# Moving the fp32-to-bf16 casts of x from GpSimd to VectorE in a scaled matrix product

## The chip, the core and the metric

The kernel runs on one core of a Trainium2 chip. The metric is the device time of one execution in microseconds (us). Before the change the median of three runs was 218.16 us (218.0 to 218.54).

## The reference

```python
batch, m, k, n = 16, 512, 1024, 768        # x: batch,m,k; weight: k,n; add_value: batch,m,n; scale 0.1; all float32
def reference(x, weight, scale, add_value):
    return (scale * np.matmul(x, weight) + add_value).astype(np.float32)
```

All batches share one weight, so this is one product of 8192 x 1024 with 1024 x 768, scaled, plus an addend of the size of the result.

## The kernel before, in words

**Tiles.** The 8192 rows are cut into T = 64 tiles of 128 rows (row number p * 64 + t is partition p of tile t, so that several tiles in a row are one contiguous piece per partition). [...]

**Memory.** `xs` is a ring of 24 slots for x tiles in fp32 (512 KB each), `ao` a ring of 24 slots for tiles of add_value (384 KB each); the result overwrites the addend in its slot and is stored from there. The weights are staged in the last eight slots of `ao` before the addends need them (L79), and kept in `w_bf` as bf16. There are four buffers for casts (`xb`), three for transposed tiles (`xt`), two for transposes in PSUM (`tp`) and three for products in PSUM (`mm`).

**What happens to one tile t.**
- It is cast from fp32 to bf16, `xb` from `xs` (L87), by `cast_to`.
- TensorE transposes it in four pieces (L97). Pairs of neighbouring bf16 values are treated as one 4-byte value, so four 128x128 transposes against an fp32 identity move the 1024 columns.
- ScalarE copies the transposes out of PSUM into `xt` and sorts the pairs apart (L99).
- TensorE does 16 matmuls into `mm` (L114): 4 chunks by 2 members of a pair by 2 column pieces.
- VectorE computes `ao` = scale * `mm` + `ao` in one instruction (L118), called the add below.
- SyncE stores `ao` (L144), usually four tiles at a time.

**What sets the order.** The instructions stand in each engine's queue in the order in which the program emits them, and each engine takes its queue in order. `STREAM` (L11 to L23) is the written order of all DMAs, all on SyncE's queue: loads of x ("x"), weights ("w"), add_value ("a") and stores ("o"), with first tile and number of tiles. The loop over it (L127) emits the work of tiles only when it is needed: before a store, all steps up to its last tile (`steps_to`), and before a load of x into a slot that is still in use, steps until the old tile there has been cast. The four weight loads and their casts on VectorE (`load_w`, L81) are emitted at once when the loop meets them, and the first steps come only with the store ("o", 0, 4).

`step` (L103) emits one tile's matmuls. After the first half of its chunks it calls `transpose(t + 1)`, so that the transposes and the copy of the next tile lie within the matmuls of this one; `transpose` calls `cast_to` for its tile (L92). The casts are on GpSimd, whose queue holds nothing else after the identity matrix is made, so that they run ahead of TensorE as far as the loads and the four `xb` buffers let them.

Of the kernel before, what the change touches and what calls it, by code (L numbers as in the profile page):

```python
# [1 line left out]

# [5 lines left out]

STREAM = [  # L11
    ("x", 0, 1), ("w", 0, 1), ("w", 1, 1), ("w", 2, 1), ("w", 3, 1), ("x", 1, 1),
    ("x", 2, 2), ("a", 0, 4), ("x", 4, 4), ("a", 4, 4), ("x", 8, 4), ("a", 8, 4),
    ("x", 12, 4), ("a", 12, 4), ("x", 16, 4), ("a", 16, 4), ("x", 20, 4), ("o", 0, 4),
    ("a", 20, 4), ("x", 24, 4), ("o", 4, 4), ("a", 24, 4), ("x", 28, 4), ("o", 8, 4),
    ("a", 28, 4), ("x", 32, 4), ("o", 12, 4), ("a", 32, 4), ("x", 36, 4), ("o", 16, 4),
    ("a", 36, 4), ("x", 40, 4), ("o", 20, 4), ("a", 40, 4), ("x", 44, 4), ("o", 24, 4),
    ("a", 44, 4), ("x", 48, 4), ("o", 28, 4), ("a", 48, 4), ("x", 52, 4), ("o", 32, 4),
    ("a", 52, 4), ("x", 56, 2), ("o", 36, 4), ("x", 58, 2), ("a", 56, 2), ("x", 60, 1),
    ("a", 58, 2), ("x", 61, 1), ("o", 40, 4), ("x", 62, 1), ("a", 60, 1), ("x", 63, 1),  # L20
    ("a", 61, 1), ("a", 62, 1), ("a", 63, 1), ("o", 44, 4), ("o", 48, 4), ("o", 52, 4),
    ("o", 56, 2), ("o", 58, 2), ("o", 60, 1), ("o", 61, 1), ("o", 62, 1), ("o", 63, 1),
]  # L23

X_SLOTS = 24
A_SLOTS = 24


@with_exitstack
def kernel(  # L30
    ctx: ExitStack,
    tc: tile.TileContext,
    x: bass.AP,
    weight: bass.AP,
    scale: float,
    add_value: bass.AP,
    out: bass.AP,
):
    nc = tc.nc
    P = 128  # L40
    bf16 = mybir.dt.bfloat16
    fp32 = mybir.dt.float32

    x_f = x.flatten_outer_dims()
    add_f = add_value.flatten_outer_dims()
    out_f = out.flatten_outer_dims()
    M, K = x_f.shape
    _, N = weight.shape
    T = M // P
    KC = K // (2 * P)  # L50

    x_v = x_f.rearrange("(p t) k -> p t k", p=P)
    add_v = add_f.rearrange("(p t) n -> p t n", p=P)
    out_v = out_f.rearrange("(p t) n -> p t n", p=P)

    w_v = weight.rearrange("(c p r) n -> p c r n", p=P, r=2)

    const = ctx.enter_context(tc.tile_pool(name="const", bufs=1))
    xb_pool = ctx.enter_context(tc.tile_pool(name="xb_pool", bufs=4))
    xt_pool = ctx.enter_context(tc.tile_pool(name="xt_pool", bufs=3))  # L60
    tp_pool = ctx.enter_context(
        tc.tile_pool(name="tp_pool", bufs=2, space=bass.MemoryType.PSUM))
    mm_pool = ctx.enter_context(
        tc.tile_pool(name="mm_pool", bufs=3, space=bass.MemoryType.PSUM))
    ctx.enter_context(tc.manual_schedule())

    identity = const.tile([P, P], fp32, name="identity")
    make_identity(nc, identity)
    xs = const.tile([P, X_SLOTS, K], fp32, name="xs")
    ao = const.tile([P, A_SLOTS, N], fp32, name="ao")  # L70
    w_bf = const.tile([P, KC, 2, N], bf16, name="w_bf")

    SPLITS = [(0, 512), (512, N)]

    xb_tiles, xt_tiles, done = {}, {}, {"cast": 0, "step": 0}

    def load_w(c):

        s = A_SLOTS - 2 * KC + 2 * c  # L79
        nc.sync.dma_start(ao[:, s:s + 2, :], w_v[:, c, :, :])  # L80
        nc.vector.tensor_copy(w_bf[:, c, :, :], ao[:, s:s + 2, :])  # L81

    def cast_to(t):
        while done["cast"] <= t:
            i = done["cast"]
            xb = xb_pool.tile([P, K], bf16, tag="xb")
            nc.gpsimd.tensor_copy(xb, xs[:, i % X_SLOTS, :])  # L87
            xb_tiles[i] = xb
            done["cast"] += 1

    def transpose(t):
        cast_to(t)  # L92

        pairs = xb_tiles.pop(t).bitcast(fp32)
        tp = tp_pool.tile([P, KC, P], fp32, tag="tp")
        for c in range(KC):
            nc.tensor.transpose(tp[:, c, :], pairs[:, c * P:(c + 1) * P], identity)  # L97
        xt = xt_pool.tile([P, KC, 2, P], bf16, tag="xt")
        nc.scalar.copy(  # L99
            xt, tp.bitcast(bf16).rearrange("p c (m r) -> p c r m", r=2))  # L100
        xt_tiles[t] = xt

    def step():  # L103
        t = done["step"]
        if t == 0:
            transpose(0)
        xt = xt_tiles.pop(t)
        mm = mm_pool.tile([P, 1024], fp32, tag="mm")
        for c in range(KC):
            if c == KC // 2 and t + 1 < T:  # L110
                transpose(t + 1)
            for r in range(2):
                for n0, n1 in SPLITS:
                    nc.tensor.matmul(  # L114
                        mm[:, n0:n1], xt[:, c, r, :], w_bf[:, c, r, n0:n1],
                        start=(c == 0 and r == 0), stop=(c == KC - 1 and r == 1))
        a = ao[:, t % A_SLOTS, :]
        nc.vector.scalar_tensor_tensor(  # L118
            a, mm[:, 0:N], float(scale), a,
            op0=mybir.AluOpType.mult, op1=mybir.AluOpType.add)  # L120
        done["step"] += 1

    def steps_to(t):
        while done["step"] <= t:
            step()

    for op, s, n in STREAM:  # L127
        if op == "w":
            load_w(s)
            continue  # L130
        last = s + n - 1
        if op == "x":
            if last >= X_SLOTS:
                while done["cast"] <= last - X_SLOTS:
                    step()
            k = s % X_SLOTS
            nc.sync.dma_start(xs[:, k:k + n, :], x_v[:, s:s + n, :])  # L137
        elif op == "a":
            k = s % A_SLOTS
            nc.sync.dma_start(ao[:, k:k + n, :], add_v[:, s:s + n, :])  # L140
        else:
            steps_to(last)
            k = s % A_SLOTS
            nc.sync.dma_start(out_v[:, s:s + n, :], ao[:, k:k + n, :])  # L144


# [1 line left out]
_INS = ['x', 'weight', 'scale', 'add_value']  # L148
_OUTS = [((16, 512, 768), 'float32')]

_NUMBERS = {'scale': 0.10000000149011612}


# [26 lines left out]
```

## Time and profile before

| what | value |
|---|---|
| median of three runs | 218.16 us |
| the profiled execution's own time | 218.0 us |
| its span, first to last instruction | 216.2 us |
| ScalarE copies (L99) | 64, mean 1012 ns |
| loads of x, 2 MB each | median 20.7 us from issue to landing |
| loads of add_value, 1.5 MB each | median 15.9 us |
| stores, 1.5 MB each | median 23.5 us |
| bytes moved | 87.23 MB, 403 GB/s over the span |

How to read it: engines are PE (TensorE's matmuls and transposes), PEld (its weight loads, beside PE), DVE (VectorE), ACT (ScalarE), POOL (GpSimd) and SP (SyncE). The page gives the busy time and the number of instructions of each engine; the span in 40 slices, each digit the busy share in tenths; the chain that ended last, which goes back from the last instruction to whatever released it, by engine and line; and groups of instructions, each with its line, engine, operation, output <- inputs, shape and count, then busy us, mean ns of one, and the idle time of the engine before them with what ended it. A row of the timeline is start us, duration us, engine, line, operation, and in brackets the idle time before it and its releaser. A row of the chain in order of time is start us, duration us, engine and line. In the slices, the DMA engines and PE are both nearly full:

```profile
PE   0739999999999999999999999999999999999991
DVE  0521333233323332233223323332233223332331
POOL 3032526162333233233332333233323332331000
PEclk9999999999999999999999999999999999999997
DMA  6999999999999999999999999999999999999733
```

### The profile page before, as it was taken

What the parts mean: (1) busy time and instruction counts of PE and PEld (TensorE: products, weight loads), DVE (VectorE), ACT (ScalarE), POOL (GpSimd) and SP (SyncE); (2) the same over time, 40 slices, a digit from 0 to 9 for tenths busy, and PEclk for the clock granted to TensorE, in tenths of its full rate; (3) what the DMA queues carried; (4) which work ended last, traced back from release to release, by engine and by line L of the source; (5) the groups of instructions that cost most, each with busy time, mean ns of one, the idle gap of its engine ahead of it and who ended that gap; (6) DMA issues with size and microseconds to landing.
All of it is one profiled execution on the core that took longest, in us unless ns stands there. A gap on an engine that the chain in (4) does not pass through costs nothing.

```text
span 216.2 us, 3116 instructions
## 1 busy us (share of the span) xinstructions
PE 200.2 (93%) x1255; PEld 124.6 (58%) x1280; DVE 65.1 (30%) x68; ACT 66.1 (31%) x65; POOL 66.8 (31%) x70
## 2 busy tenths in 40 slices
PE   0739999999999999999999999999999999999991
PEld 0325665666566656666666566656666666666650
DVE  0521333233323332233223323332233223332331
ACT  2112223322333233323332333233323332333220
POOL 3032526162333233233332333233323332331000
PEclk9999999999999999999999999999999999999997
DMA  6999999999999999999999999999999999999733
GB/s 229 421 430 430 430 422 445 412 427 417 433 434 421 432 428 426 420 430 435 422 422 436 420 433 419 446 411 435 419 436 420 416 421 421 418 434 418 303 121 146
DMA packets 9518, 87.23 MB, mean 403 GB/s; under 512 B 1056, under 2 KB 1056, under 8 KB 3872
## 3 DMA queue, kind: packets, MB, share of 16 engines
q1 hardware_dynamic: 9504, 87.04, 95.6%
q8 instruction: 10, 0.16, 0.3%
q14 instruction: 4, 0.03, 0.0%
HBM read 61.87 MB, written 25.17 MB: 403 GB/s over the span
## 4 chain that ended last, share of the span: by engine, by line
PE 90%; DMA 4%; SPq 1%; issue 1%; POOL 0%; ACT 0%; DVE 0%; ACTq 0%
PE mm L114 77%; PE tp L97 13%; DMA xs<-in_x_dram 4%; SPq L80 1%; POOL xb L87 0%; ACT xt L99 0%; DVE ao L118 0%; SPq L137 0%; ACTq L99 0%
## 5 line engine op out<-in xcount | busy, mean ns | idle before, releaser
L114 PE MATMUL mm<-w_bf,xt 128*128 128x512 bf16 (+1 forms) x999 | 181.2, 329 | 2.6 <-ACT xt L99 1.3
L114 PEld LDWEIGHTS <-xt 128*128 128x128 bf16 x1024 | 96.1, 99 | 69.8 <-ACT xt L99 16.9
L99 ACT COPY xt<-tp 128x1024 bf16<-128x1024 bf16 x64 | 64.8, 1012 | 142.3 <-PE tp L97 142.3
L87 POOL CAST xb<-xs 128x1024 bf16<-128x1024 f32 x64 | 66.1, 1041 | 129.4 <-PE tp L97 97.4
L118 DVE SCALAR_TENSOR_TENSOR ao<-mm,ao 128x768 f32<-128x768 f32 x64 | 61.3, 957 | 138.8 <-PE mm L114 132.3
L97 PE MATMUL tp<-identity,xb 128*128 128x128 f32 x256 | 39.4, 278 | 9.1 <-POOL xb L87 9.1
L97 PEld LDWEIGHTS tp<-identity,xb 128*128 128x128 f32 x256 | 30.4, 143 | 17.1 <-POOL xb L87 9.8
L81 DVE CAST w_bf<-ao 128x1536 bf16<-128x1536 f32 x4 | 3.8, 959 | 9.0 <-DMA ao<-in_weight_dram 9.0
L99 ACT ACT_TABLE_LOAD x1 | 1.3, 1283 | 0.7 <-PEq L161 0.7
masks.py:199 POOL TENSOR_SCALAR_AFFINE_SELECT identity<-identity 128x128 f32<-128x128 f32 x1 | 0.3, 292 | 0.1
masks.py:197 POOL MEMSET identity<- 128x128 f32 x1 | 0.2, 204 | 0.3 <-POOLq L161 0.3
L161 POOL MEMSET const-float32-0.0<- 128x1 f32 x1 | 0.1, 98 | 0.2 <-issue 0.2
L161 POOL MEMSET const-bfloat16-1.0<- 128x1 bf16 x1 | 0.1, 101 | 0.0
L161 POOL MEMSET const-uint8-127<- 128x1 uint8 x1 | 0.1, 101 | 0.0
L161 POOL MEMSET const-float32-1.0<- 128x1 f32 x1 | 0.1, 98 | 0.0
## 6 DMA issues: line engine op xcount, KB each, us to landing
xs<-in_x_dram SPq DMA_DIRECT2D x13, 2048.0 KB, 20.7
ao<-in_add_value_dram SPq DMA_DIRECT2D x14, 1536.0 KB, 15.9
out_dram<-ao SPq DMA_DIRECT2D x14, 1536.0 KB, 23.5
xs<-in_x_dram SPq DMA_DIRECT2D x6, 512.0 KB, 14.8
ao<-in_weight_dram SPq DMA_DIRECT2D x4, 768.0 KB, 7.1
xs<-in_x_dram SPq DMA_DIRECT2D x3, 1024.0 KB, 17.8
ao<-in_add_value_dram SPq DMA_DIRECT2D x2, 768.0 KB, 15.3
ao<-in_add_value_dram SPq DMA_DIRECT2D x4, 384.0 KB, 13.4
```

Of the source, the lines that this page charges most:

```text
L80: nc.sync.dma_start(ao[:, s:s + 2, :], w_v[:, c, :, :])
L81: nc.vector.tensor_copy(w_bf[:, c, :, :], ao[:, s:s + 2, :])
L87: nc.gpsimd.tensor_copy(xb, xs[:, i % X_SLOTS, :])
L97: nc.tensor.transpose(tp[:, c, :], pairs[:, c * P:(c + 1) * P], identity)
L99: nc.scalar.copy(xt, tp.bitcast(bf16).rearrange("p c (m r) -> p c r m", r=2))
L114: nc.tensor.matmul(mm[:, n0:n1], xt[:, c, r, :], w_bf[:, c, r, n0:n1], start=(c == 0 and r == 0), stop=(c == KC - 1 and r == 1))
L118: nc.vector.scalar_tensor_tensor(a, mm[:, 0:N], float(scale), a, op0=mybir.AluOpType.mult, op1=mybir.AluOpType.add)
L161: nc = _bacc.Bacc("TRN2", target_bir_lowering=False, num_devices=1)
```

## The change

The casts of x are issued on VectorE instead of GpSimd, and `step` calls `cast_to(t + 2)` before the add of tile t. Nothing else in the text of the kernel changes: the order of the DMAs, the number of buffers, the transposes and the matmuls are as before. In the built program the queue of VectorE holds four weight casts, then the casts of tiles 0, 1 and 2, the add of tile 0, the cast of tile 3, the add of tile 1, the cast of tile 4 and so on; GpSimd's queue ends with the identity matrix. The queues of TensorE, ScalarE and SyncE hold the same instructions in the same order; where they waited for GpSimd's casts they now wait for VectorE's.

```diff
@@ cast_to
             xb = xb_pool.tile([P, K], bf16, tag="xb")
-            nc.gpsimd.tensor_copy(xb, xs[:, i % X_SLOTS, :])
+            nc.vector.tensor_copy(xb, xs[:, i % X_SLOTS, :])
             xb_tiles[i] = xb
@@ step
                         mm[:, n0:n1], xt[:, c, r, :], w_bf[:, c, r, n0:n1],
                         start=(c == 0 and r == 0), stop=(c == KC - 1 and r == 1))
+        if t + 2 < T:
+            cast_to(t + 2)
         a = ao[:, t % A_SLOTS, :]
         nc.vector.scalar_tensor_tensor(
```

## The prediction

> **What bounds the kernel now.** I read the page first: busy shares, the chain, the groups.
>
> ```profile
> PE 200.2 (93%) x1255; PEld 124.6 (58%) x1280; DVE 65.1 (30%) x68; ACT 66.1 (31%) x65; POOL 66.8 (31%) x70
> PE mm L114 77%; PE tp L97 13%; DMA xs<-in_x_dram 4%; SPq L80 1%; POOL xb L87 0%; ACT xt L99 0%; DVE ao L118 0%; SPq L137 0%; ACTq L99 0%
> L87 POOL CAST xb<-xs 128x1024 bf16<-128x1024 f32 x64 | 66.1, 1041 | 129.4 <-PE tp L97 97.4
> L118 DVE SCALAR_TENSOR_TENSOR ao<-mm,ao 128x768 f32<-128x768 f32 x64 | 61.3, 957 | 138.8 <-PE mm L114 132.3
> L97 PE MATMUL tp<-identity,xb 128*128 128x128 f32 x256 | 39.4, 278 | 9.1 <-POOL xb L87 9.1
> L81 DVE CAST w_bf<-ao 128x1536 bf16<-128x1536 f32 x4 | 3.8, 959 | 9.0 <-DMA ao<-in_weight_dram 9.0
> ```
>
> TensorE carries 90% of the chain. The casts and the adds are off it (0% each); both engines spend most of their time waiting for PE. But PE's only waits for a cast (9.1 us, the L97 row) must lie somewhere, and the chain in order of time says where: at the start.
>
> ```profile
> 3.35 9.71 DMA xs<-in_x_dram
> 13.12 1.05 POOL xb L87
> 14.21 1.12 PE tp L97 x4
> 15.33 4.63 PE mm L114 x16
> 19.96 0.44 PE tp L97 x4
> 20.40 2.28 PE mm L114 x14
> ```
>
> From 14.21 us on PE never stops: one tile is 2.63 (16 matmuls) + 0.44 (4 transposes) = 3.07 us, repeated to 211.9. A 0.3 us slip near 110 is the only other gap. The sum: 14.21 us of start, PE's work, then 4.3 us of last add, store and closing (211.9 to 216.2). The timeline shows what PE did before 14.21:
>
> ```profile
> 4.33 1.04 POOL L87 CAST xb<-xs 128x1024 bf16<-128x1024 f32 x1 [3.03 <-DMA xs<-in_x_dram]
> 5.42 1.12 PE L97 MATMUL tp<-identity,xb 128*128 128x128 f32 x4 [5.42 <-POOL xb L87]
> 6.57 1.01 ACT L99 COPY xt<-tp 128x1024 bf16<-128x1024 bf16 x1 [4.55 <-PE tp L97]
> 7.64 2.86 PE L114 MATMUL mm<-w_bf,xt 128*128 128x512 bf16 x8 [1.10 <-ACT xt L99]
> 11.84 0.96 DVE L81 CAST w_bf<-ao 128x1536 bf16<-128x1536 f32 x1 [0.89 <-DMA ao<-in_weight_dram]
> ```
>
> Tile 0's cast, transposes, eviction and first 8 matmuls fit into the time in which the weights and x tile 1 were still arriving. That free work is what the change touches. The last view is the weight loads around 19 us, where two loads stand for one pair of matmuls (512 and 256 columns):
>
> ```profile
> 14.91 0.36 PEld L114 LDWEIGHTS <-xt 128*128 128x128 bf16 x2
> 15.55 0.36 PEld L114 LDWEIGHTS <-xt 128*128 128x128 bf16 x2 [0.28 <-issue]
> 18.75 0.36 PEld L114 LDWEIGHTS <-xt 128*128 128x128 bf16 x2 [0.28 <-issue]
> 19.36 0.21 PEld L114 LDWEIGHTS <-xt 128*128 128x128 bf16 x2 [0.25 <-issue]
> 19.69 0.47 PEld L97 LDWEIGHTS tp<-identity,xb 128*128 128x128 f32 x4
> ```
>
> Pairs are 0.64 us apart (15.55 - 14.91) until about 19.4, then 0.33 us (19.69 - 19.36; in steady state 2.63 / 8). So PE runs at half speed until some 4.4 us after its long run of matmuls began (15.12 in the timeline); its first burst, 7.64 to 10.5, was all slow. The page's clock row reads 9 throughout and does not show this.
>
> **The change, part by part.**
>
> *The 64 casts leave GpSimd.* That frees 64 x 1.04 us there. POOL's cast leads PE by several tiles from 24 us on and delays nothing, so this is worth 0. Nothing disturbed these casts either: the shortest took 1036 ns, the longest 1041.
>
> *They join VectorE.* No row shows a VectorE cast of 1024 columns. The nearest is its own cast of 1536 columns, same types: 959 ns. In proportion that is 0.64 us; it can't exceed 0.96. I take 0.70, nearer the proportional end, as a small fixed part is likely; the ends move the result by -0.06 and +0.26 us. [...] Per tile VectorE then has 0.96 + 0.70 = 1.66 us of work in 3.07, so it does not become the bound.
>
> *The steady state.* VectorE's order becomes add t, cast t+3, add t+1. Add 3 ends at 27.85 + 0.96 = 28.81, so cast 6 runs 28.81 to 29.51; transposes 6 start at 32.05 in the same trace. Spare: 2.5 us per tile, 0 cost. Without that cover each late microsecond would count some 60 times. A cast that waits for x would hold the add behind it: heads of loads arrive at 24.29 (tile 4), 34.34 (8), 42.93 (12), 51.51 (16) by the POOL waits, while cast 4 can't start before add 1 ends, some 25.1 with the shift below, and casts 8, 12, 16 later still (37 us and on). So no new wait. Adds keep their time after their matmuls; the three mm buffers come free as before.
>
> *SyncE.* Slot waits for x now look at VectorE's casts, up to 8 us later than POOL's. The x load of tiles 24 to 27 went out at 37.95 and needs casts 0 to 3, done by some 23; the later ones have over 20 us of margin (tiles 28 to 31: issued 64.1, casts 4 to 7 done by 35). Stores go out later by PE's shift; the loads of add_value behind them wait for a store's landing (63.67 for tiles 24 to 27), land some 16 us later, about 80, and are used at 92. 12 us cover a shift of 2 to 4. Cost 0.
>
> *The start, which pays.* VectorE is in order and the four weight casts stand ahead of cast 0. The last of these waits for its weights until 11.84 and ends at 12.80. So cast 0 moves from 4.33 to 12.80, and ends at 13.50; transposes at 13.55 (0.05 as in 14.16 to 14.21). Then with the rows above:
> - slow transposes 0: 1.12, to 14.67; eviction until the first matmul 1.10 (6.54, where the transposes of 5.42 end, to 7.64), to 15.77. Nothing covers this, since no other tile is ready.
> - first half of tile 0, 4 pairs x 0.64 = 2.56, to 18.33; transposes 1, slow (14.21 to 15.12), 0.91, to 19.24. Cast 1 is done at 14.2, cast 2 at 16.3 (x landed at 15.6).
> - second half of tile 0: full speed, by the 4.4 us above, at 15.77 + 4.4 = 20.17. The first 0.93 us do half work, 0.47 of 1.32; the other 0.85 ends at 21.02.
> - first half of tile 1: 1.32, to 22.34; transposes 2: 0.44, to 22.78.
>
> The old chain had the same work behind it at 20.40. The shift is 22.78 - 20.40 = **+2.4 us**, and PE, which has no gap later, hands it all to the end. The terms: half a tile that was free is now paid (1.3), eviction and transposes of tile 0 too (2.2 slow), less what the earlier start and the slow time saved give back.
>
> The row gives the moment of full speed once only. Lower end: full speed from the first matmul at 15.77: 1.32 + 0.44 + 1.32 + 1.32 + 0.44 = 4.84, to 20.61, +0.2. At the same moment as now (19.5): +2.05. Upper end: the transposes break the run and the 4.4 us begin anew at 19.24, so full speed at 23.64: second half slow to 21.80, of the next half 1.84 us do 0.92 and 0.40 remain, 24.04, transposes 24.48: +4.1. I take +2.4, the delay of the row counted from the first matmul.
>
> [...]
>
> **The sum.** The profiled execution took 218.0 us, span 216.2 and 1.8 around it; 218.0 + 2.4 = **220.4 us**. The median of three is 0.16 above that run, well inside the range.
>
> **Rivals.**
> - *Late full speed* (transposes 1 break the run): +2.9 to +4.1, 220.9 to 222.1. For it: the burst at 7.64 to 10.5, with its weight waits, stayed slow. Against: in steady state transposes between matmuls cost no speed.
> - *Early full speed*: below +1.9, 218.2 to 219.9. For it: nothing but that one row is all we have. Against: both first bursts were slow.
> - *The start is absorbed* (not slower): if the transfers, not PE, set the end, PE would catch up in later waits and the time stays at 218.0. For it: the DMA row is at 9 to slice 37, and 427 GB/s over 1.31 MB per tile is 3.07 us too. It decides once PE's waits for x after 20 us reach 2.4 us; the trace has none, and after 200 us DMA falls to half load, waiting for adds. GpSimd's absence would have to speed up something PE waits for, to be faster; no row shows such a thing.
> - *Casts late in every tile*: needs a cast over 0.70 + 2.5 = 3.2 us, when VectorE's 4.2 us replace PE's 3.07 (+1.1 x 61 = 67 us, 285). A POOL cast of the same tile at 1.04 us already leaves 2.2 us.
>
> **How the numbers follow.** Forecast (+1.9 to +2.9, 219.9 to 220.9) 0.60; late full speed 0.20; early 0.10; absorbed 0.05; casts late or other new waits 0.05. The range, 219.5 to 222.1, holds the first two and some of the early case. A measurement can tell 0.3%, 0.65 us. Slower by more: 0.60 + 0.20 + 0.05 + 0.08 of the early case = 0.93; within: 0.02 of the early case and 0.03 of the absorbed = 0.05; faster: 0.02.
>
> **What would show it.** The first transposes at 13.5 instead of 5.4, first matmul near 15.8; PE's wait for a cast one long one at the start and none later; VectorE's cast row x64 near 700 ns; the pair spacing falling to 0.33 near 20.2; the chain 3.07 per tile; last matmul near 214.3; closing 4.3 us. Casts appearing as PE's releaser after 25 us, or a VectorE cast waiting for x past tile 4 with the add behind it late, would make me wrong.

## The result, and the profile after

The changed kernel took 220.35 us (median of four, 220.0 to 221.31), the kernel before 218.35 us beside it (218.0 to 218.57): a ratio of 1.010, 95% interval 1.0062 to 1.0138. The forecast was 220.4. The profiled executions differ by the same: 220.0 against 218.0, spans 218.2 against 216.2.

The page of the changed kernel: its busy row, the chain by line, and the transposes and casts.

```profile
PE 197.5 (91%) x1255; PEld 123.9 (57%) x1280; DVE 103.6 (47%) x132; ACT 66.1 (30%) x65; POOL 0.7 (0%) x6
PE mm L114 77%; PE tp L97 13%; DMA ao<-in_weight_dram 4%; ACT xt L99 1%; SPq L80 1%; DVE w_bf L81 0%; DVE ao L120 0%; DVE xb L87 0%; SPq L139 0%; ACTq L99 0%
L97 PE MATMUL tp<-identity,xb 128*128 128x128 f32 x256 | 39.1, 276 | 13.8 <-DVE xb L87 13.8
L87 DVE CAST xb<-xs 128x1024 bf16<-128x1024 f32 x64 | 43.6, 683 | 1.6 <-DMA xs<-in_x_dram 1.6
```

VectorE's busy share goes from 30% to 47% and this costs nothing. What tells is the third line's idle time: PE's waits for casts grew from 9.1 to 13.8 us, and in the chain the transfer at the start is now that of the weights, not of x. The view of waits says how often:

```profile
PE tp L97 <- DVE xb L87: 13.8, 1, 13.8
DVE xb L87 <- DMA xs<-in_x_dram: 1.6, 1, 1.6
```

The columns are us in total, times, longest. One wait of PE in the whole execution, the first; after it the casts never make PE wait. The same chain in order of time, from the last weights on:

```profile
2.58 9.49 DMA ao<-in_weight_dram
12.07 0.02 issue
12.10 0.96 DVE w_bf L81
13.06 0.61 DVE xb L87
13.67 0.14 issue
13.80 1.10 PE tp L97 x4
14.90 0.02 issue
14.93 1.02 ACT xt L99
15.95 0.05 issue
15.99 2.74 PE mm L114 x8
18.74 0.64 PE tp L97 x4
19.37 2.60 PE mm L114 x16
21.97 0.44 PE tp L97 x4
```

Cast 0 stands behind the last weight cast. Transposes 2 end at 22.41, against 20.40 before: 2.01 us. The last matmuls, first in the kernel before, then in the changed one:

```profile
207.95 3.95 PE mm L114 x24
209.96 3.95 PE mm L114 x24
```

They end at 213.91 against 211.90: 2.01 us again. So all of the difference is there by the third tile, and nothing is lost or won in the 190 us after it. The timeline shows why the steady state holds:

```profile
29.86 0.96 DVE L120 SCALAR_TENSOR_TENSOR ao<-mm,ao 128x768 f32<-128x768 f32 x1 [1.52 <-PE mm L114]
30.73 0.68 DVE L87 CAST xb<-xs 128x1024 bf16<-128x1024 f32 x1
33.95 0.47 PEld L97 LDWEIGHTS tp<-identity,xb 128*128 128x128 f32 x4
```

These are add 3, cast 6 and the start of transposes 6: the cast ends at 31.41, 2.5 us before it is needed.

### The profile page after: what moved, and what is told of

It reads as the page before. It is cut to its first block, busy times and chain, and to the rows that moved or that the text cites. A ratio compares the mean times of both kernels' runs of the same rounds, so it can differ in the third digit from the quotient of the medians.

```text
span 218.2 us, 3041 instructions
## 1 busy us (share of the span) xinstructions
PE 197.5 (91%) x1255; PEld 123.9 (57%) x1280; DVE 103.6 (47%) x132; ACT 66.1 (30%) x65; POOL 0.7 (0%) x6
## 4 chain that ended last, share of the span: by engine, by line
PE 90%; DMA 4%; DVE 1%; issue 1%; ACT 1%; SPq 1%; ACTq 0%
PE mm L114 77%; PE tp L97 13%; DMA ao<-in_weight_dram 4%; ACT xt L99 1%; SPq L80 1%; DVE w_bf L81 0%; DVE ao L120 0%; DVE xb L87 0%; SPq L139 0%; ACTq L99 0%
## 5 line engine op out<-in xcount | busy, mean ns | idle before, releaser
L114 PE MATMUL mm<-w_bf,xt 128*128 128x512 bf16 (+1 forms) x999 | 179.0, 327 | 2.6 <-ACT xt L99 1.3
L97 PE MATMUL tp<-identity,xb 128*128 128x128 f32 x256 | 39.1, 276 | 13.8 <-DVE xb L87 13.8
L87 DVE CAST xb<-xs 128x1024 bf16<-128x1024 f32 x64 | 43.6, 683 | 1.6 <-DMA xs<-in_x_dram 1.6
## 6 DMA issues: line engine op xcount, KB each, us to landing
xs<-in_x_dram SPq DMA_DIRECT2D x6, 512.0 KB, 15.1
```

The costliest lines, as they stand in the source:

```text
L87: nc.vector.tensor_copy(xb, xs[:, i % X_SLOTS, :])
L114: nc.tensor.matmul(mm[:, n0:n1], xt[:, c, r, :], w_bf[:, c, r, n0:n1], start=(c == 0 and r == 0), stop=(c == KC - 1 and r == 1))
```

## The experiments

The theory: the loss is the start alone, since cast 0 waits in VectorE's in-order queue behind four weight casts. The rival: VectorE as the place of the casts costs something in every tile. "Before" times beside the runs were 217.9 to 218.2.

**1. Cast 0 back to GpSimd.**

```diff
-            nc.vector.tensor_copy(xb, xs[:, i % X_SLOTS, :])
+            eng = nc.gpsimd if i == 0 else nc.vector
+            eng.tensor_copy(xb, xs[:, i % X_SLOTS, :])
```

> Cast 0 alone goes back to GpSimd, the other 63 stay on VectorE. Theory (the start pays all): tile 0's first half is free work again; cast 1 follows the last weight cast at about 13.06 and ends at 13.74, so transposes 1 start near 13.8 instead of 14.21 in the kernel before: span 216.2 - 0.4 = 215.8, time 217.6 us. Rival (the casts on VectorE cost something in every tile): the time stays at 220.0.

Measured: 217.61 us, ratio to the kernel before 0.998 (0.9965 to 0.9996). One cast out of 64 takes the whole loss back. Transposes 1 started at 14.11, not 13.8, as x tile 1 landed at 13.33 in this execution.

**2. Cast 0 alone on VectorE, in the kernel before.**

```diff
-            nc.gpsimd.tensor_copy(xb, xs[:, i % X_SLOTS, :])
+            eng = nc.vector if i == 0 else nc.gpsimd
+            eng.tensor_copy(xb, xs[:, i % X_SLOTS, :])
```

> The kernel before with cast 0 alone on VectorE, the other 63 on GpSimd. Theory (the start pays all): this one cast, held behind the last weight cast until 13.06, costs as much as the whole change: 220.0 us, within 0.7 for the moment of full speed. Rival (the cost is in the steady state): 218.2, as the kernel before.

Measured: 219.99 us, ratio 1.009 (1.007 to 1.011). The chain is that of the changed kernel:

```profile
13.05 0.61 DVE xb L88
13.66 0.14 issue
13.80 1.10 PE tp L98 x4
```

One cast moved makes the whole loss. With run 1, from the other side, the rival is out.

**3. Cast 0 on VectorE, ahead of the weight casts.**

```diff
             nc.sync.dma_start(xs[:, k:k + n, :], x_v[:, s:s + n, :])
+            if s == 0:
+                cast_to(0)
```

> The changed kernel with cast 0 emitted right after its load, so that it stands ahead of the weight casts in VectorE's queue. Theory (the place in the in-order queue, not the engine, is what cost): cast 0 at 4.3, done at 5.0, transposes 0 at 5.1, weight casts not delayed (first weights land at 6.2); transposes 1 near 13.8: 217.6 us. Rival (VectorE itself is the wrong engine, or the cost is per tile): 220.0.

Measured: 217.65 us, ratio 0.9978 (0.9966 to 0.999). All 64 casts on VectorE, and slightly faster than before: the place in the queue cost, not the engine. In its chain the cast of tile 1 takes 0.70 us, 1.05 before (a row under 0.1 us left out):

```profile
13.34 0.70 DVE xb L87
14.09 1.11 PE tp L97 x4
15.20 4.38 PE mm L114 x16
```

The profiled execution started transposes 1 at 14.09 (before: 14.21), as x tile 1 landed 0.25 us later than before, and was done with the 16 matmuls sooner (4.38 for 4.63). The shorter cast is worth 0.35 us; that the 0.2% are this and not the moment of full speed is argued, not shown.

**4. Casts one tile ahead instead of two.**

```diff
-        if t + 2 < T:
-            cast_to(t + 2)
```

> The changed kernel without the line that casts two tiles ahead: cast t+1 stands right before add t. Theory (a spare of 2.5 us per tile, of which one tile's 3.07 us is taken): cast ends 0.87 + 0.68 + 0.1 = 1.65 us after an add starts, transposes want to start 1.13 after it, so 0.52 us of wait in each of 62 tiles: 220.0 + 32 = 252 us. Rival (the steady state has more room than I think, for instance because the order across engines adapts): 220.

Measured: 257.42 us (one execution), 37.4 above the changed kernel. The chain of one tile:

```profile
28.48 0.03 DVE ao L118
28.52 0.84 issue
29.36 0.69 DVE xb L87
30.05 0.14 issue
30.19 0.63 PE tp L97 x4
30.82 1.31 PE mm L114 x8
32.13 0.02 issue
32.15 0.97 DVE ao L118
```

The add starts at 28.48 and the next at 32.15: 3.67 us a tile instead of 3.07, and 62 x 0.60 = 37.2. Of the 0.60, 0.41 is PE's wait (38.8 us in all, less the 13.8 at the start, over 61), and 0.19 comes from the transposes, which take 0.63 after a wait and 0.44 in an unbroken run. The expectation had only a wait, of 0.52 us. So the line with t + 2 is what makes the change affordable: the order is at the edge of a cliff, 2.5 us of spare against 3.07 for one tile.

**The size of the start loss** depends on when TensorE reaches full speed. The changed kernel was run again for this.

> The changed kernel once more, for the moment of full speed. If it is counted from the first matmul (4.4 us in the kernel before, 2.7 in the changed one: these already disagree), no prediction; if the moment falls by chance in a window of some 3 us, the time follows it at one half: time = 220.0 + (moment - 18.7) / 2, between 219.9 and 221.4. Rival (the moment is fixed in the span, near 18.7 us): 220.0 again.

Measured: 220.99 us. In the first execution the weight loads of PE turn close just after transposes 1:

```profile
17.68 0.36 PEld L114 LDWEIGHTS <-xt 128*128 128x128 bf16 x2 [0.28 <-issue]
18.32 0.81 PEld L97 LDWEIGHTS tp<-identity,xb 128*128 128x128 f32 x4 [0.28 <-issue]
19.10 1.18 PEld L114 LDWEIGHTS <-xt 128*128 128x128 bf16 x8
```

In the second one they are still far apart after these transposes:

```profile
19.50 0.36 PEld L114 LDWEIGHTS <-xt 128*128 128x128 bf16 x2
20.14 0.36 PEld L114 LDWEIGHTS <-xt 128*128 128x128 bf16 x2 [0.28 <-issue]
20.74 1.83 PEld L114 LDWEIGHTS <-xt 128*128 128x128 bf16 x12 [0.24 <-issue]
```

Eight loads in 1.18 us are full speed, two in 0.64 half speed. So full speed comes during transposes 1 in the one and near 20.7 in the other. Each trace also records the granted clock, from its first release to full speed on: this release is at 19.01 us in the one and at 20.69 in the other (the expectation had read 18.7 for the first). Transposes 2 end at 23.40 instead of 22.41: 0.99 us, and the time is 0.99 us longer. Of this 0.33 is the start (the last weight cast at 12.42 for 12.10). The rest is the moment of full speed: from the first matmul on, half speed lasted 3.02 us in the one and 4.37 in the other, and half of the difference is 0.67. That the expectation's formula, without the start and with 18.7, also gives 1.0 is luck; its window of some 3 us was an estimate of the author's, and the two moments lie 1.68 us apart.

From the first matmul of the long run this moment was 4.2 us off in the kernel before, 3.0 and 4.4 in the two executions here, 2.7, 3.5 and 3.7 in runs 2, 1 and 3: not a constant. What sets it isn't shown. In both executions full speed lasted 197.97 us, 58 times 3.413. Counted back from 19.01 and 20.69 in such steps, the first matmul (15.99 and 16.32) stood 0.4 us behind the start of a step in the one and 2.5 us in the other. This is an estimate, as nothing is recorded before the first release.

**5 to 7. Keeping TensorE busy with dummy matmuls while it waits.** Dummies multiply the identity's bytes with themselves into a PSUM tile that nobody reads; `warm(n)` issues n of them.

```diff
+    def warm(n):
+        wt = tp_pool.tile([P, KC, P], fp32, tag="tp")
+        ib = identity.bitcast(bf16)
+        for _ in range(n):
+            nc.tensor.matmul(wt[:, 0:2, :], ib[:, 0:P], ib, start=True, stop=True)
...
         if t == 0:
+            warm(80)
             transpose(0)
```

> The changed kernel with 80 dummy matmuls (128x256, identity by itself, into a PSUM tile that nobody reads) in the time in which TensorE waits for cast 0. Theory (the slow speed after 14 us is a matter of recent activity, and part of the 2 us): transposes 0 at 13.80, 0.44 + 1.10 to the first matmul, then 1.32 + 0.44 + 1.32 + 1.32 + 0.44, so transposes 2 end at 20.2 instead of 22.4: 220.0 - 2.2 = 217.8 us. Rival (the slow speed comes from the loads or from something else than activity): 220.0, or later where the dummies run on beyond 13.8.

Measured: 219.81 us (218.82 to 220.83), no clear gain over 220.35. The profiled execution has transposes 0 at full speed (0.67 us from 13.55), and then pairs 0.64 apart from 15.72 to 21: between the dummies' end at 11.58 and the first matmul at 15.72 PE was busy for 0.7 of 4.1 us and lost its speed. Here the clock row does show it, in the third and fourth slices (10.9 to 21.9 us):

```profile
PEclk9985999999999999999999999999999999999999
```

The next two have 18 dummies before transposes 0 and 14 before transposes 1, with cast 0 first on VectorE (run 6) and in the kernel before (run 7).

> Cast 0 first on VectorE, as in the run with cast 0 ahead of the weight casts (217.65), with 18 dummy matmuls before transposes 0 and 14 before transposes 1. Theory: from 14.09 the chain is 0.44 + 1.32 + 1.32 + 0.44, transposes 2 end at 17.6 instead of 20.0: 217.65 - 2.4 = 215.2 us, faster than both kernels. Rival (not a matter of activity): 217.65.

Measured: 217.4 us, ratio 0.997 (0.9958 to 0.9983). Full speed was kept and matmuls after transposes 2 began at 17.58, as expected; yet of the 2.4 us only 0.25 reached the end. The chain of this kernel tells why (rows under 0.1 us left out):

```profile
4.89 19.39 DMA xs<-in_x_dram
24.38 0.70 DVE xb L87
25.08 0.14 issue
25.21 0.63 PE tp L97 x4
```

The load of x tiles 4 to 7 lands as a whole at 24.28, and transposes 4 wait for it. A second wait lies before: cast 3 stands behind add 0, which waits for its addend until 19.49, so transposes 3 start at 21.19 instead of 20.2.

> The kernel before with the same 18 and 14 dummy matmuls. Theory: from 14.21 the chain is 0.44 + 1.32 + 1.32 + 0.44, transposes 2 end at 17.7 instead of 20.4: 218.2 - 2.7 = 215.5 us, so the casts' engine is worth 0.3 between this and the last kernel, by the shorter cast of tile 1. Rival: 218.2.

Measured: 218.35 us, but from 217.63 to 220.72 and once 222.1: no gain, and a scatter that no run without dummies had. In the profiled execution PE idled 2.8 us before transposes 1, and the granted clock was at half from 14.8 to 18.2; tile 4 landed at 24.25 here too. Where the longest times come from isn't known.

**8 to 11. Taking the next waits away.** The load is split, and on VectorE casts run three tiles ahead.

```diff
-    ("x", 2, 2), ("a", 0, 4), ("x", 4, 4),
+    ("x", 2, 2), ("a", 0, 4), ("x", 4, 1), ("x", 5, 1), ("x", 6, 2),
...
-        if t + 2 < T:
-            cast_to(t + 2)
+        if t + 3 < T:
+            cast_to(t + 3)
```

> Cast 0 first, dummy matmuls (18 and 22), and the two waits that ate the gain in the run with 18 and 14 taken away: the load of x tiles 4 to 7 is issued as 1, 1 and 2 tiles, so that tile 4 lands near 20.5 instead of 24.3, and casts run three tiles ahead, so that cast 3 does not stand behind add 0, which waits for its addend until 19.4. Theory: transposes 1 at 14.05, transposes 2 end at 17.6, no wait after: 217.65 - 2.4 = 215.2 us. Rival (a further load is late, or the transfers now set the end): 216.5 to 217.4.

Run 8 measured 216.17 us (215.5 to 216.7), ratio to the kernel before 0.9909 (0.9887 to 0.993): faster than both kernels. In the profiled execution (216.62) the speed had gone down early, so that the dummies themselves ran slow and held up transposes 1 until 15.1:

```profile
7.47 0.64 PEld L123 LDWEIGHTS <-xt 128*128 128x128 bf16 x4 [0.25 <-issue]
10.37 4.63 PEld L107 LDWEIGHTS <-identity 128*128 128x128 bf16 x22 [0.28 <-issue]
```

Read in stretches of 3.41 us (from:to and length; busy time and number of instructions of PE, PEld, DVE, ACT and POOL; granted clock; DMA share; GB/s):

```profile
5.01:8.42 3.41, 1.72 (x10) 0.90 (x9) 1.34 (x3) 1.01 (x1) 0.00 (x0) 1.00 1.02 427
8.42:11.84 3.42, 2.49 (x10) 1.43 (x10) 1.84 (x2) 0.00 (x0) 0.00 (x0) 0.50 1.00 418
11.84:15.25 3.41, 3.41 (x18) 2.39 (x16) 1.66 (x2) 0.00 (x0) 0.00 (x0) 0.50 1.08 449
15.25:18.66 3.41, 3.41 (x26) 2.32 (x25) 1.30 (x2) 1.01 (x1) 0.00 (x0) 1.00 0.97 410
```

Transposes 2 end at 18.90, 1.3 us later than expected, and no wait follows.

> The same kernel without the dummy matmuls. Theory (the two waits exist only once TensorE is ahead of the loads): as the run with cast 0 first alone, 217.65 us. Rival (the split load itself is what gains): 215 to 216.

Run 9 measured 217.93 us (216.77 to 218.44), ratio 0.9989 (0.9972 to 1.0006): the split and the third tile are worth nothing while TensorE is behind the loads.

> The changed kernel with 96 dummy matmuls ahead of transposes 0 and 9 more between them and the first matmul, so that TensorE is idle for no more than some 0.5 us there; with 80 and no others it went slow again at 15.3 to 15.7, after 2.0 and 1.5 us of idle time with 0.7 us of transposes between. Theory (those gaps lost the full speed): transposes 2 end at 20.2: 217.8 us. Rival (dummies do not keep the speed): 219.8 as with 80.

Run 10 measured 218.75 us (218.74 to 218.93). The matmuls behind transposes 2 begin at 20.19 in its timeline, as expected, and full speed was kept: from 11 to 18 us PE was busy for 6.88 of 7 us, at a granted clock of 1.00. Then tile 4, which landed at 25.7, takes about 1 us back. It landed 1.4 us later than in run 6, and so did tiles 2 and 3 (17.1 for 15.7); why is open.

> The kernel before, casts on GpSimd, with the split load and the dummy matmuls (18 and 22). Theory: transposes 1 at 14.3 (GpSimd's cast of 1.04 instead of 0.70 us), transposes 2 end at 17.9: 218.1 - 2.5 = 215.6 us, so that the engine of the casts is worth 0.3 to 0.4 us once its place in the queue is right. Rival (the full speed is lost in the 2 us gap before transposes 1): 217.5 to 218.

Run 11 measured 215.9 us (215.75 to 216.54), ratio 0.9909 (0.989 to 0.9927), the same as with the casts on VectorE. The expected advantage of VectorE, 0.3 to 0.4 us, can't be seen; the profiled executions of runs 8 and 11 both had slow dummies that held up transposes 1, which covers the shorter cast.

## Why the prediction was right

- *The steady state costs nothing*: right, with the spare of 2.5 us as forecast. Run 4 shows what it is worth.
- *The cast takes 0.70 us*: 0.683 measured, 0.04 above the proportional end of 0.64. A fixed part by itself no run shows.
- *SyncE's waits, the late slot release*: no wait of a cast on x but one of 1.6 us (tile 2), and every tile from the third on at the old pace.
- *The start pays all of it*: right, shown from both sides by runs 1 and 2, and 3 shows that the queue order is the cause.
- *The size*: +2.4 forecast, +2.0 by both pairs of medians and profiles. Two terms were off, in opposite directions. Transposes 0 began at 13.80, not 13.55, since the last weights came 0.26 us later, and their first eight matmuls took 2.74, not 2.56: 0.4 us more. "Full speed, by the 4.4 us above, at 15.77 + 4.4 = 20.17" is the step that does not hold: it came at 19.01, 3.0 us behind the first matmul and not 4.4, and the three terms behind the first eight matmuls took 3.68 us (0.64, 2.60, 0.44) for 4.45. That is 0.8 us less. That the one takes back half of the other is luck: in the second execution the moment does come 4.4 us behind the first matmul, the later start stays, and the time is 220.99. One row had been read as a fixed delay; over the executions above it varies from 2.7 to 4.4 us. The +1.9 at which the forecast's interval begins, and the early case ends, was the author's estimate, and no run of the changed kernel shows it: its two traced executions had +2.0 and +3.0.
- *The rival of late full speed*: met in neither traced execution (19.0 and 20.7, against its 23.64), though 220.99 lies in its range of times by the later start; the one at 221.31 has no trace.
- *The rival of an absorbed start*: out. PE had no gap to catch up in. But its mechanism is real from the other side: once the start was 2.4 us shorter (run 6), loads took most of it back.

## What to carry to other kernels

When work moves to another engine, look first at what its queue holds before the first moved instruction: here a weight cast that waited for its transfer until 12.10 us held cast 0 until 13.06, and this one place was the whole cost, 2.0 us, while the added busy time was free. Price the distance at which work is issued ahead against the period of the loop, since one step less turned no cost into 0.60 us per tile here. And when a start gets shorter, ask which transfer is next to be late before counting the gain (in run 6 the load that landed at 24.28 us).

## What the runs showed of the hardware

- The clock row read 9 during the slow phase at the start of both kernels (pairs 0.64 us apart), but fell to 8 and 5 where full speed had once been reached and was lost (run 5). The record behind the row has no entry before the first release. The spacing of the weight loads tells both.
- The granted clock changed in steps of one length. Full speed lasted from 19.33 to 213.89 us in the kernel before, 57 times 3.413 us, and 197.97 us in both executions of the changed kernel, 58 times; in run 8 the clock is full from 5.01 to 8.42, half to 15.25 and full to 213.22, which is 1, 2 and 58 times.
- Full speed was lost after short gaps. In run 8 PE had gaps of 1.4 and 1.1 us around four matmuls at full speed; in the stretch to 8.42 it was busy for 1.72 us, and half speed followed. In run 6 about the same gaps did not matter: the steps lay otherwise, and PE was busy for 1.59 us in the stretch from 6.56 to 9.97. So the busy time alone does not decide. The first stretch held four transposes (0.66 us), the second none; whether that is the reason isn't shown. Where speed was lost between two matmuls, the longest idle time was 2.8 us (run 7).
- In the changed kernel VectorE started the next cast 0.87 us after an add that is shown with 0.96 us (30.73 for 29.86), and casts 0 and 1 lay 0.6 us apart, less than the 0.68 shown for one.
